# The first MLP's down projection in seven products, with the residual kept in DRAM

## The chip, the cores and the metric

The kernel runs on one core of a Trainium2 chip. The metric is device time in microseconds (us) for one execution; lower is better. Five engines work side by side and meet through semaphores: TensorE (PE; its weight loads are listed apart as PEld), VectorE (DVE), ScalarE (ACT), GpSimd (POOL) and SyncE (SP), which issues most transfers.

## What is computed

A trunk of two layers over 512 tokens of width 1024, all in float32. Each layer is a mixer (latent attention in layer 0, gated linear attention, "GLA", in layer 1) and an MLP, each added to the residual stream `x`; a last RMS norm follows. The change is in the MLP of layer 0.

```python
D_MODEL = 1024; SEQ = 512; D_FF = 4 * D_MODEL

def sq_relu_mlp(xn, w_up, w_down):
    hid = jnp.square(jax.nn.relu(xn @ w_up))
    return hid @ w_down

for i in range(DEPTH):
    ...
    x = x + mix.astype(x.dtype)
    x = x + sq_relu_mlp(rms_norm(x, norm_mlp[i]), mlp_w_up[i], mlp_w_down[i]).astype(x.dtype)
return rms_norm(x, final_norm)
```

## The kernel before

**Precision.** A float32 matrix is split into a rounded high part (ACT copies it, line 104) and a low part (DVE subtracts, line 107). A product takes three matmuls: high x high, high x low, low x high. Weights pass through `piece`, which has three buffers for high parts (`wh`) and three for low (`wl`).

**The stream.** `xT` is one SBUF tile, `xall`, of 128 partitions x 8 x 512: the residual with features on the partitions and tokens along the row.

**MLP of layer 0, `mlp` (from line 799).** The 4096 hidden features are done in eight blocks of 512. The first block's up projection, `up`, is plain: 96 matmuls of 512 columns. The other seven are made by `up_fast`: the 1024 x 512 weight block and the activations are cut into 2 x 2 quadrants, and seven products of sums of quadrants (Winograd's form of Strassen's scheme) replace eight. Each product is 8 matmuls of 512 columns (line 891; high and low activations side by side) and 8 of 256 (line 892). The down projection of every block, `down`, is plain: 8 output tiles, 12 matmuls of 512 columns each (lines 112 to 114), each tile added to `xT` by DVE (line 843). `down` of block b is woven into `up_fast` of block b + 1 through `others`. So seven periods of one fast up step and one plain down block follow `up`, and the eighth `down` stands alone at the end; there `nxt.add` scales each finished tile for the next norm, and GLA begins.

**MLP of layer 1, `mlp_last` (from line 972).** Here both projections use seven products. A step, `step`, alternates up products (24 matmuls of 256 columns, line 1108) with down products (12 of 512 columns, line 1117). A down product's output has tokens on the partitions. Partial results are summed in five tiles: S11, S12, SU, S21, which lie over `xall`, and S5. Since they lie over the residual, `residual` first turns it by 32 TensorE transposes (line 1061) into the sums. The quadrants of activations and their combinations T1 to T4 (`quadrants`) are made in four buffers of the pool `comb`, then rounded into tiles `T`; the buffers then serve for weights. `home` says which buffer a weight quadrant gets: d11, d12, d22 and so on are quadrants of `w_down`, dS1 and dS3 sums of two (the second added in flight by an accumulating transfer from POOL), S1 such a sum of `w_up`, A1 and A2 halves of `w_up` in the buffers `wraw`. `fetch` issues the loads. The step's parts of hidden quadrants are split into four pairs of tiles, `parts_room`. After seven steps the eighth block is plain, with the output norm woven in.

**Order.** A scheduler orders each engine's instructions at build time from the program; in a queue nothing overtakes. PSUM has eight banks: in `mlp` z and y (two each), three for `down` and one; in `mlp_last` four for up products (`u`) and d and e (two each) for down products.

Of the kernel before, what the change touches and what calls it, by code (L numbers as in the profile page):

```python
# [50 lines left out]
def trunk_kernel(ctx: ExitStack, tc: tile.TileContext, t_in: dict, out: bass.AP):  # L51
# [47 lines left out]
    def f(ap):  # L99
        return ap.bitcast(F32)  # L100
# [698 lines left out]
    def mlp(layer, nrm, tag, nxt):  # L799
        w_up, w_dn = t_in["mlp_w_up"][layer], t_in["mlp_w_down"][layer]  # L800
        X = nrm.out
        NB = FF // FB

        es = ExitStack()
        fast = es.enter_context(tc.tile_pool(name=f"fast{layer}", bufs=1, reuse_waits="tile"))

        def up():
            hid = []
            for c in range(2):
                raw = col_chunk(w_up, c * 256, 256)  # L810
                w = [piece(raw[:, :, j * P : (j + 1) * P], ND, P) for j in range(2)]
                ps_ = split_banks("zy"[c])
                if c == 0:
                    a_pair(ps_, w, nrm)
                else:
                    for j in range(2):
                        a_type(ps_[j], w[j], X)
                for j in range(2):
                    r = tmp()
                    DVE.scalar_tensor_tensor(r, ps_[j], 0.0, nrm.rstd, ALU.max, ALU.mult)  # L820
                    q = tmp()
                    ACT.activation(q, r, AF.Square)
                    hi, lo = slot(tag), slot(tag)
                    ACT.activation(hi, q, AF.Copy)
                    quad["hid"] = DVE.tensor_tensor(lo, q, f(hi), ALU.subtract).ins
                    hid.append((hi, lo))
            return hid

        def down(b, hid):
            for c in range(2):  # L830
                src = w_dn[b * FB : (b + 1) * FB, c * 512 : (c + 1) * 512].rearrange("(k p) n -> p k n", p=P)
                if c == 0 and b < NB - 1:
                    raw = fast.tile([P, 4, 512], F32, tag="raw", name=uname("raw"))
                    SP.dma_start(raw, src)
                else:
                    raw = load(src, 4, 512)
                for g in range(2):
                    w = piece(raw[:, :, g * 256 : (g + 1) * 256], 4, 256)
                    for j in range(2):
                        m = c * 4 + g * 2 + j  # L840
                        p = bank("b")
                        a_type(p, w, hid, cols=slice(j * P, (j + 1) * P))
                        DVE.tensor_tensor(xT[m], p, xT[m], ALU.add)
                        if b == NB - 1:
                            nxt.add(m, xT[m])
                        yield

        first, second = slice(0, TH), slice(TH, S)  # L850
        KH = ND // 2

        def comb():
            return fast.tile([P, KH, 256], F32, tag="comb", bufs=4, name=uname("comb"))

        quad = {}

        def quadrants():
            lead, trail = range(KH), range(KH, ND)
            quad["11"] = [nrm.parts[k][:, :, first] for k in lead]  # L860
            quad["21"] = [nrm.parts[k][:, :, first] for k in trail]
            quad["22"] = [nrm.parts[k][:, :, second] for k in trail]
            t1, t2, t3, t4 = comb(), comb(), comb(), comb()
            for k in lead:
                g1, g2 = (gcol(nrm.g, nrm.g0 + j) for j in (k, k + KH))
                u, v = xT[k], xT[k + KH]
                ACT.activation(t3[:, k], u[:, second], AF.Copy, scale=g1)
                DVE.scalar_tensor_tensor(t3[:, k], v[:, second], g2, t3[:, k], ALU.mult, ALU.subtract)
                DVE.scalar_tensor_tensor(t2[:, k], u[:, first], g1, t3[:, k], ALU.mult, ALU.add)
                DVE.scalar_tensor_tensor(t4[:, k], v[:, first], g2, t2[:, k], ALU.mult, ALU.subtract)  # L870
                DVE.scalar_tensor_tensor(t1[:, k], v[:, second], g2, t2[:, k], ALU.mult, ALU.subtract)
            for name, t in (("T2", t2), ("T3", t3), ("T1", t1), ("T4", t4)):
                parts = fast.tile([P, KH, 2, TH], F32R, tag=name, name=uname(name))
                split(t, parts[:, :, 0], parts[:, :, 1])
                quad[name] = [parts[:, k] for k in lead]

        def up_fast(b, others):
            raw = [col_chunk(w_up, b * FB + c * 256, 256) for c in range(2)]
            a11, a12 = raw[0][:, :KH], raw[0][:, KH:]
            a21, a22 = raw[1][:, :KH], raw[1][:, KH:]  # L880
            halves = [(slot(tag), slot(tag)) for _ in range(4)]


            def product(t, a, q, start):
                w = piece(a, KH, 256)
                for j in range(2):
                    o = t[:, j * 512 : (j + 1) * 512]
                    for k in range(KH):
                        wh, wl = cut(w, slice(None), k, slice(j * P, (j + 1) * P))
                        x = quad[q][k]  # L890
                        PE.matmul(o.rearrange("p (h t) -> p h t", h=2), wh, x, start=start and k == 0, stop=False, skip_group_check=True)  # L891
                        PE.matmul(o[:, :TH], wl, x[:, 0], start=False, stop=k == KH - 1, skip_group_check=True)  # L892

            def parts(t):
                v = t.rearrange("p (j h t) -> p h j t", j=2, h=2)
                return v[:, 0], v[:, 1]

            def by_tile(v):
                return v.rearrange("p (j t) -> p j t", j=2)


            def total(t, term=None):
                high, low = parts(t)
                r = tmp()
                if term is None:
                    ACT.activation(by_tile(r), low, AF.Copy)
                else:
                    DVE.tensor_tensor(by_tile(r), low, by_tile(term), ALU.add)
                DVE.tensor_tensor(by_tile(r), high, by_tile(r), ALU.add)
                return r  # L910


            def finish(c, half, tk):
                c3 = by_tile(c)
                DVE.scalar_tensor_tensor(c3, c3, 0.0, nrm.rstd[:, tk].unsqueeze(1).to_broadcast([P, 2, TH]), ALU.max, ALU.mult)
                ACT.activation(c, c, AF.Square)
                for j in range(2):
                    hi, lo = halves[2 * half + j]
                    split(c3[:, j], hi[:, tk], lo[:, tk])

            z, y = two_banks("z"), two_banks("y")
            product(z, a11, "11", True)
            others(1)
            p1 = total(z)
            s1, s2 = comb(), comb()
            DVE.tensor_tensor(s1, a21, a22, ALU.add)
            DVE.tensor_tensor(s2, s1, a11, ALU.subtract)
            product(y, a12, "21", True)
            c11 = total(y, p1)
            product(z, s2, "T2", False)  # L930
            others(2)
            u = total(z)
            finish(c11, 0, first)
            s4 = comb()

            with tc.issue_after(quad["hid"]) if b == 1 else nullcontext():
                DVE.tensor_tensor(s4, a12, s2, ALU.subtract)
                DVE.tensor_tensor(a21, a11, a21, ALU.subtract)
            product(z, a21, "T3", False)
            v = total(z)  # L940
            y = two_banks("y")
            product(y, s1, "T1", True)
            others(1)
            c22 = total(y, v)
            product(y, s4, "22", False)
            product(z, a22, "T4", False)
            finish(c22, 1, second)
            c12 = total(y, u)
            finish(c12, 0, second)
            c21 = total(z)  # L950
            finish(c21, 1, first)
            others(4)
            return halves

        hid = up()
        quadrants()
        for b in range(NB):
            if b + 1 < NB:
                tiles = down(b, hid)

                def others(n):
                    for _ in range(n):
                        next(tiles)

                hid = up_fast(b + 1, others)
                continue
            es.close()
            for _ in down(b, hid):
                pass
# [890 lines left out]
```

## Time and profile before

| | us |
|---|---|
| median of 3 runs | 1069.12 (1068.77 to 1069.77) |
| profiled execution | 1070.06 |
| its span, first to last instruction | 1068.4 |
| layer 0: first up block ends | 205.59 |
| layer 0: last plain down block begins | 495.48 |
| layer 1: first up block ends | 761.33 |
| layer 1: last plain block begins | 1039.82 |

The granted TensorE clock is 0.999 of full on the mean. By DMA queue, packets, megabytes and the share of the sixteen DMA engines' time:

```profile
q1 hardware_dynamic: 89376, 106.22, 30.6%
q0 software_dynamic: 11200, 14.68, 8.6%
```

q1 is SP's queue, q0 POOL's. A line number in the profile is a line of the kernel before; lines 104 and 107 are in a helper, so tiles tell such rows apart (`wh<-wraw`, `wh<-comb`). A matmul's duration includes its way through the array, and consecutive matmuls overlap.

### The profile page before, as it was taken

The numbers are of one execution on the slowest core, as the hardware profiler recorded it, in microseconds if no ns is written. First come the engines' busy times: TensorE is split into PE (matmuls) and PEld (weight loads), VectorE is DVE, ScalarE is ACT, GpSimd is POOL, SyncE is SP. The second block draws the span as 40 slices with busy tenths as digits, with TensorE's granted clock in tenths as the row PEclk, the third lists the DMA queues.
The fourth block names the chain that finished last, engine by engine and source line by source line (L and its number), as shares of the span: only waits on it lengthen the run. The fifth ranks groups of instructions, "written<-read, shape, count | busy, mean of one in ns | idle before, by whom it ended". The sixth has DMA issues, their size and how long they took to land.

```text
span 1068.4 us, 14750 instructions
## 1 busy us (share of the span) xinstructions
PE 1058.9 (99%) x5626; PEld 908.2 (85%) x5626; DVE 868.1 (81%) x1384; ACT 630.2 (59%) x1010; POOL 78.5 (7%) x100
## 2 busy tenths in 40 slices
PE   9999999999999999999999999999999999999997
PEld 8888888888888888888888888878889999999985
DVE  7899977987978878877778389478789989989993
ACT  7667654553444444445445475665567767777784
POOL 8310002000000000000000000000011011010000
PEclk9999999999999999999999999999999999999999
DMA  7311223142233233214222221343576786696622
GB/s 228 89 50 40 80 83 114 40 157 80 79 124 113 79 111 114 92 41 154 73 98 62 97 64 47 116 101 127 138 208 149 196 236 137 180 252 142 176 82 79
DMA packets 102742, 123.67 MB, mean 116 GB/s; under 512 B 8368, under 2 KB 74416, under 8 KB 102672
## 3 DMA queue, kind: packets, MB, share of 16 engines
q1 hardware_dynamic: 89376, 106.22, 30.6%
q0 software_dynamic: 11200, 14.68, 8.6%
q10 hardware_dynamic: 2096, 1.84, 0.5%
q8 instruction: 44, 0.72, 0.3%
q14 instruction: 26, 0.21, 0.1%
HBM read 120.37 MB, written 2.10 MB: 115 GB/s over the span
## 4 chain that ended last, share of the span: by engine, by line
PE 93%; DVE 3%; ACT 2%; DMA 1%; issue 1%; ACTq 0%; DVEq 0%
PE ps L112 15%; PE ps L114 15%; PE ps L113 15%; PE ps L1108 13%; PE ps L1117 13%; PE ps L891 8%; PE ps L892 4%; PE ps L1504 2%; PE ps L129 1%; PE ps L1284 1%; PE ps L408 1%; DMA comb<-in_mlp_w_down_dram 1%; PE ps L1631 1%; DVE wl L107 1%; DVE T L999 0%
## 5 line engine op out<-in xcount | busy, mean ns | idle before, releaser
L104 ACT ACTIVATE wh<-wraw 128x1024 fp32r<-128x1024 f32 x139 | 146.6, 1058 | 153.3 <-PE ps L113 73.8
L112 PE MATMUL ps<-set,wh 128*128 128x512 f32 x536 | 209.1, 391 | 0.5 <-ACT set L1673 0.3
L113 PE MATMUL ps<-set,wh 128*128 128x512 f32 x536 | 209.2, 391 | 0.0
L114 PE MATMUL ps<-set,wl 128*128 128x512 f32 x536 | 208.7, 390 | 0.0
L107 DVE TENSOR_TENSOR wl<-wraw,wh 128x1024 fp32r<-128x1024 f32 x139 | 169.6, 1222 | 34.8 <-ACT wh L104 34.6
L1117 PE MATMUL ps<-wh,set 128*128 128x512 f32 x392 | 129.3, 390 | 0.0
L104 ACT ACTIVATE wh<-comb 128x1024 fp32r<-128x1024 f32 x77 | 81.8, 1062 | 75.0 <-PE ps L891 40.9
L107 DVE TENSOR_TENSOR wl<-comb,wh 128x1024 fp32r<-128x1024 f32 x77 | 94.2, 1223 | 36.2 <-ACT wh L104 36.1
L112 PEld LDWEIGHTS ps<-set,wh 128*128 128x128 f32 x536 | 100.6, 188 | 22.2 <-ACT wh L104 1.0
L114 PEld LDWEIGHTS ps<-set,wl 128*128 128x128 f32 x536 | 100.6, 188 | 21.6 <-DVE wl L107 0.4
L113 PEld LDWEIGHTS ps<-set,wh 128*128 128x128 f32 x536 | 100.7, 188 | 19.7
L1117 PEld LDWEIGHTS ps<-wh,set 128*128 128x128 f32 x392 | 73.7, 188 | 14.4
L1108 PE MATMUL ps<-T,wh 128*128 128x256 f32 x448 | 79.9, 279 | 0.0
L891 PE MATMUL ps<-T,wh 128*128 128x512 f32 x224 | 78.7, 391 | 0.0
L1117 PE MATMUL ps<-wl,set 128*128 128x512 f32 x196 | 76.8, 392 | 0.0
L1108 PEld LDWEIGHTS ps<-T,wh 128*128 128x128 f32 x448 | 70.3, 188 | 2.2
L892 PE MATMUL ps<-T,wl 128*128 128x256 f32 x224 | 63.1, 282 | 0.0
L1108 PE MATMUL ps<-T,wl 128*128 128x256 f32 x224 | 62.6, 279 | 0.5 <-DVE wl L107 0.5
L1108 PE MATMUL ps<-set,wh 128*128 128x256 f32 x336 | 61.3, 283 | 0.0
L891 PE MATMUL ps<-set,wh 128*128 128x512 f32 x168 | 60.0, 397 | 0.0
L112 PE MATMUL ps<-wh,set 128*128 128x512 f32 x144 | 58.6, 407 | 0.0
L114 PE MATMUL ps<-wh,set 128*128 128x512 f32 x144 | 56.8, 396 | 0.0
(416 smaller groups left out, 2205.6 us busy)
## 6 DMA issues: line engine op xcount, KB each, us to landing
wraw<-in_mlp_w_up_dram SPq DMA_DIRECT2D x32, 1024.0 KB, 5.4
comb<-in_mlp_w_down_dram SPq DMA_DIRECT2D x39, 512.0 KB, 4.7
wraw<-in_gla_w_in_dram SPq DMA_DIRECT2D x12, 1024.0 KB, 5.2
wraw<-in_mlp_w_down_dram SPq DMA_DIRECT2D x9, 1024.0 KB, 5.1
raw<-in_mlp_w_down_dram SPq DMA_DIRECT2D x7, 1024.0 KB, 5.0
comb<-in_mlp_w_down_dram POOLq DMA_DIRECT2D x14, 512.0 KB, 7.3
wraw<-in_mla_w_o_dram SPq DMA_DIRECT2D x4, 1024.0 KB, 5.3
wraw<-in_gla_w_o_dram SPq DMA_DIRECT2D x4, 1024.0 KB, 5.5
```

The lines of the kernel that those rows point to most:

```text
L104: order(ACT.activation(hi, src, AF.Copy))
L107: lo_eng.tensor_tensor(lo, src, f(hi), ALU.subtract)
L112: PE.matmul(psum, wh, xh, start=start, stop=False)
L113: PE.matmul(psum, wh, xl, start=False, stop=False)
L114: PE.matmul(psum, wl, xh, start=False, stop=stop)
L129: PE.transpose(psum, src, ident[: src.shape[0], : src.shape[0]])
L408: PE.matmul(p, w[:, i, j * P : (j + 1) * P], x, start=start, stop=stop)
L891: PE.matmul(o.rearrange("p (h t) -> p h t", h=2), wh, x, start=start and k == 0, stop=False, skip_group_check=True)
L892: PE.matmul(o[:, :TH], wl, x[:, 0], start=False, stop=k == KH - 1, skip_group_check=True)
L1108: PE.matmul(o, a_, x_, start=start and j == 0 and k == 0 and n == 0, stop=k == KH - 1 and n == 2, skip_group_check=True)
L1117: PE.matmul(o, x_, w_, start=start and k == 0 and n == 0, stop=k == 1 and n == 2, skip_group_check=True)
L1504: PE.matmul(p[:, t - t0], k[:, t * P : (t + 1) * P], moving[:, t], start=True, stop=True)
```

## The change

`mlp` is removed, and `mlp_last`, now called `mlp`, serves both layers; it is told by `nxt` that a norm follows. For layer 0:

- PSUM has the layout of layer 1 (`"quad"`).
- `residual` is not called. SP stores `xall` in a DRAM tile, `x_kept`, of 128 x 8 x 512, ahead of dS3's load. In the first step the sums are not added to but written (`opening`).
- In the last step, four loads bring `x_kept` back, two tiles at a time, into `comb` buffers, and two load the last block's down weights into `wraw`.
- The last block is plain, with features on the partitions again. The parts of the hidden quadrants are laid in `room` with all 512 tokens of a tile in a row. For every output tile four transposes turn the sums' 128 x 128 pieces into its bank, and 12 matmuls of 512 columns add the block's product onto them; DVE adds the kept residual, and `nxt.add` follows.

For both layers, d11 and dS3 exchange their first buffers.

```diff
-    def mlp(layer, nrm, tag, nxt):
...
-    def mlp_last(layer, nrm):
+    def mlp(layer, nrm, nxt=None):
...
+        if nxt:
+            dram = es.enter_context(tc.tile_pool(name=f"spill{layer}", bufs=1, space=bass.MemoryType.DRAM))
+            x_kept = dram.tile([P, ND, S], F32, name="x_kept")
...
-        home = {"S1": 0, "dS1": 1, "d11": 2, "d12": 3, "dS3": 4, "d22": 5}
+        home = {"S1": 0, "dS1": 1, "d11": 4, "d12": 3, "dS3": 2, "d22": 5}
...
         def step(b, q, r, after):
+            opening = b == 0 and nxt is not None
...
             def add(total, t):
-                DVE.tensor_tensor(total, t, total, ALU.add)
+                if opening:
+                    ACT.activation(total, t, AF.Copy)
+                else:
+                    DVE.tensor_tensor(total, t, total, ALU.add)
...
             down_product(d, d11, parts_of_quad(q11), True)
-            e = begun(d)
+            if opening:
+                ACT.activation(S11, d, AF.Copy)
+            e = two_banks("e") if opening else begun(d)
...
-            down_product(e, d12, parts_of_quad(q21), False)
-            add(S11, e)
+            down_product(e, d12, parts_of_quad(q21), opening)
+            DVE.tensor_tensor(S11, e, S11, ALU.add)
...
-            onto("d", S21, d22, parts_of_quad(q21, -1.0))
+            onto("d", S21, d22, parts_of_quad(q21, -1.0), opening)
...
-        residual()
+        if not nxt:
+            residual()
         for name in ("S1", "dS1", "d11", "A1", "d12", "dS3", "A2", "d22"):
-            fetch(0, name)
+            if name == "dS3" and nxt:
+                with tc.issue_after(queued.ins):
+                    SP.dma_start(x_kept, xall)
+            queued = fetch(0, name)
...
+        def before_next(name):
+            if name in ("d11", "S1", "d12", "dS3"):
+                t = by_k(comb(home[name]), 2)
+                SP.dma_start(t, x_kept[:, 2 * len(kept) : 2 * len(kept) + 2])
+                kept.append(t)
+            if name in ("A1", "A2"):
+                last_raw.append(load(down_cols(len(last_raw)), 4, 512))
+            if name == "dS1":
+                DVE.tensor_tensor(S12, S12, S5, ALU.add)
...
+        if nxt:
+            room = [parts_room[(turn[0] + k) % 4] for k in range(4)]
+            for h, th in ((0, 0), (0, 1), (1, 1), (1, 0)):
+                for j in range(2):
+                    split(q[h][th][:, j * TH : (j + 1) * TH], *cut(room[2 * h + j], slice(None), (first, second)[th]))
+            DVE.scalar_tensor_tensor(S21, S21, -1.0, SU, ALU.mult, ALU.subtract)
+            DVE.scalar_tensor_tensor(SU, SU, -1.0, S5, ALU.mult, ALU.subtract)
+            for c in range(2):
+                ps_ = [bank("u") for _ in range(4)] if c == 0 else [p for tag in "ed" for p in split_banks(tag)]
+                for j, p in enumerate(ps_):
+                    for t in range(NT):
+                        o = t % 2 * 512 + j * P
+                        src = (S11, S12, S21, SU)[2 * c + t // 2][:, o : o + P]
+                        PE.matmul(p[:, t * P : (t + 1) * P], src, ident, start=t == 0, stop=False, is_transpose=True, skip_group_check=True)
+                for j, p in enumerate(ps_):
+                    if j % 2 == 0:
+                        w = piece(last_raw[c][:, :, j * P : (j + 2) * P], 4, 256)
+                    for k in range(4):
+                        wh, wl = cut(w, slice(None), k, slice(j % 2 * P, (j % 2 + 1) * P))
+                        for n, (a, x) in enumerate(((wh, room[k][0]), (wh, room[k][1]), (wl, room[k][0]))):
+                            PE.matmul(p, a, x, start=False, stop=k == 3 and n == 2, skip_group_check=True)
+                    m = 4 * c + j
+                    DVE.tensor_tensor(xT[m], p, kept[m // 2][:, m % 2], ALU.add)
+                    nxt.add(m, xT[m])
+            es.close()
+            return
...
-    psum_layout(True)
-    mlp(0, n_mlp0, "B", n_mix1)
+    psum_layout("quad")
+    mlp(0, n_mlp0, n_mix1)
     psum_layout(False)
...
-    mlp_last(1, n_mlp1)
+    mlp(1, n_mlp1)
```

Three places show what the engines are given now. (Rows: line, operation, tile written <- tiles read, shape, semaphores waited for; lines after the change are those of the changed kernel.) First SP's queue at the start of layer 0. Before, with the two halves of `w_up` for the first fast step last:

```order
L834 DMA raw_2392<-in_mlp_w_down_dram 128x4x512 [waits DVE_49,PE_49,Pool_49]
L134 DMA wraw_2054<-in_mla_w_o_dram 128x8x256 [waits DMAHW6_49,DVE_49]
L134 DMA wraw_2159<-in_mlp_w_up_dram 128x8x256 [waits DMAHW7_49,DVE_49]
L134 DMA wraw_2247<-in_mlp_w_up_dram 128x8x256 [waits DMAHW1_49,DVE_49]
L134 DMA wraw_2358<-in_mlp_w_up_dram 128x8x256 [waits DMAHW2_49,DVE_49]
L134 DMA wraw_2360<-in_mlp_w_up_dram 128x8x256 [waits DMAHW3_49,DVE_49]
```

After, where wraw_2372 is A1, comb_2370 d11, comb_2374 d12, comb_2377 dS3, wraw_2380 A2 and comb_2383 d22:

```order
L134 DMA wraw_2372<-in_mlp_w_up_dram 128x8x256 [waits DMAHW3_49,DVE_49]
L926 DMA comb_2370<-in_mlp_w_down_dram 128x2x512 [waits DVE_49]
L926 DMA comb_2374<-in_mlp_w_down_dram 128x2x512 [waits DVE_49]
L1054 DMA x_kept<-xT 128x4096 [waits DMAHW0_49]
L926 DMA comb_2377<-in_mlp_w_down_dram 128x2x512 [waits DMAHW1_49,DVE_49,Pool_49]
L134 DMA wraw_2380<-in_mlp_w_up_dram 128x8x256 [waits DMAHW4_49,DVE_49]
L926 DMA comb_2383<-in_mlp_w_down_dram 128x2x512
```

The store stands between d12's load and dS3's. Second, ACT in the first step of layer 0. Before, at the first fast up step (wh_2442 and wh_2506 are weights of the following products):

```order
L906 ACTIVATE tmp_2412<-ps_532_2370 128x512 [waits PE_49]
L104 ACTIVATE wh_2442<-comb_2416 128x1024
L104 ACTIVATE wh_2476<-raw_2392 128x1024 [waits DVE_49,PE_49]
L104 ACTIVATE wh_2506<-wraw_2360 128x1024 [waits DVE_49,DMAHW5_49,PE_49,Activation_49]
L906 ACTIVATE tmp_2494<-ps_532_2370 128x512 [waits PE_49]
```

After; the row of line 985 is the copy of the first down product to S11, which lies in `xT`, and wh_2491 is the weights of the product on T2:

```order
L104 ACTIVATE wh_2471<-comb_2374 128x1024 [waits DMAHW7_49,PE_49]
L980 ACTIVATE ps_2414<-ps_2385 128x512 [waits PE_49]
L104 ACTIVATE set_2170<-set_2163 128x512 [waits DVE_49,PE_49]
L985 ACTIVATE xT<-ps_540_2416 128x1024 [waits DMAHW0_49,PE_49]
L104 ACTIVATE wh_2491<-wraw_2372 128x1024
```

The copy waits for a transfer (the store) and for TensorE, and T2's weights are queued behind it. Third, TensorE at the end of the last step of layer 0, after the change (ps_902 is bank d, ps_5124 to ps_5127 are four banks `u`, the sets are room pieces):

```order
L948 MATMUL ps_902_5087<-wh_5089,set_2171 128x512
L1122 MATMUL ps_5124<-ident,xT 128x128 x2
L1122 MATMUL ps_5124<-ident,xT 128x128 [waits DVE_49]
L1122 MATMUL ps_5124<-ident,xT 128x128
L1122 MATMUL ps_5125<-ident,xT 128x128 x4
L1122 MATMUL ps_5126<-ident,xT 128x128 x4
L1122 MATMUL ps_5127<-ident,xT 128x128 [waits DVE_49]
L1122 MATMUL ps_5127<-ident,xT 128x128 x3
L1129 MATMUL ps_5124<-set_2172,wh_5144 128x512 [waits Activation_49]
L1129 MATMUL ps_5124<-set_2173,wh_5144 128x512
```

The 16 transposes of the first four tiles stand between the last down product and the plain block; the 16 of the other four stand between the block's two halves. Before, the eighth `down` followed the seventh fast step directly. From GLA on, each engine's order is unchanged, but for SP's at the start of layer 1, where d11's load now stands ahead of d12's, d22's and dS3's, and for the lines' numbers.

More of the change, by code (lines that the diff above doesn't have):

```diff
@@ L796, in out_proj @@
                 add(m, p)
-    def mlp(layer, nrm, tag, nxt):
[L800 to L969, printed above, removed]
@@ L1095, in fetch @@
             }[name]
-            SP.dma_start(t, q(b, *plain))
+            first_part = SP.dma_start(t, q(b, *plain))
             if more:
                 POOL.dma_start(t, q(b, *more), accum_op=ALU.add)
+            return first_part
         def up_product(t, a, q, start):
@@ L1224, in rounded, with down_cols @@
                     last[c].append((parts[:, 0], parts[:, 1]))
+        def down_cols(c):
+            return w_dn[(NB - 1) * FB :, c * 512 : (c + 1) * 512].rearrange("(k p) n -> p k n", p=P)
+        def before_next(name):
[7 more added lines that the diff above has]
+                DVE.tensor_tensor(S12, S12, S5, ALU.add)
         def at_the_end(name):
@@ L1245, in after @@
                 if final:
-                    return at_the_end(name)
+                    return before_next(name) if nxt else at_the_end(name)
                 new = NEXT[name]
```

4 lines of the change are left out of this document (2 added, 2 removed).

## The prediction, made before the change was run

> **What bounds the kernel now.** I read the page's busy shares first, then busy time by stretch, then single matmuls on the timeline, and last the chain of waits. The page:
>
> ```profile
> PE 1058.9 (99%) x5626; PEld 908.2 (85%) x5626; DVE 868.1 (81%) x1384; ACT 630.2 (59%) x1010; POOL 78.5 (7%) x100
> ```
>
> TensorE never rests, but a row's duration is not its price. In the timeline of TensorE (start, duration, line), at the first seven-product up step of layer 0:
>
> ```profile
> 205.59 0.39 PE L891 MATMUL ps<-set,wh 128*128 128x512 f32 x1
> 205.82 0.28 PE L892 MATMUL ps<-set,wl 128*128 128x256 f32 x1
> 205.93 0.40 PE L891 MATMUL ps<-set,wh 128*128 128x512 f32 x1
> ```
>
> The first matmul is shown with 0.39 us, yet the next starts 0.23 us later and the one after that 0.11 us later: matmuls overlap. The price is the distance between starts, some 0.23 us for 512 columns and 0.12 us for 256. So what counts is how many columns each MLP block streams, and whether TensorE gets them without a gap. Stretches (length, busy time and count by engine, clock, DMA share, GB/s): seven blocks of layer 0 (from the matmul at 205.59 to the start of the last plain block at 495.48), and the same work of layer 1 from 783.28 to 1039.82.
>
> ```profile
> 205.59:495.48 289.89, 289.89 (x1457) 246.32 (x1456) 237.98 (x317) 132.03 (x194) 0.99 (x2) 1.00 0.30 99
> 783.28:1039.82 256.54, 256.54 (x1657) 233.93 (x1657) 231.81 (x257) 189.41 (x238) 28.80 (x23) 1.00 0.70 181
> ```
>
> No TensorE idle in either, at full clock. Layer 0 takes 289.89 / 7 = 41.41 us for a block. In layer 1 the chain of waits shows what a seven-product step is made of (start, length, what):
>
> ```profile
> 783.28 2.80 PE ps L1108 x24
> 786.08 2.75 PE ps L1117 x12
> ...
> 1037.07 2.75 PE ps L1117 x12
> 1039.82 14.03 PE ps L1284 x60
> ```
>
> An up product of 24 matmuls with 256 columns, then a down product of 12 with 512, alternating to the end with nothing between them: 46 pairs in 256.54 us, 5.577 us each. A step has seven pairs, 39.04 us. DVE is 90% busy there (231.81 of 256.54) and still does not hold TensorE up.
>
> **The change, part by part.**
>
> *Seven steps of layer 0.* Now a block is 152 matmuls of 512 columns (96 down, 56 up) and 56 of 256; after, 84 of 512 and 168 of 256. In columns that is 92,160 against 86,016, and 41.41 against 39.04 us. Layer 0 runs the code that layer 1 runs now, and the order of instructions within a step is the same; its 49 pairs cost 49 x 5.577 = 273.3 us in place of 289.89: **-16.6**. Bounds: 5.55 to 5.61 us for a pair (both spellings of the up product occur in the chain, 2.80 and 2.87), so ±1.5.
>
> On a rule of the skill: the Trainium skill, "TensorE: Matmul & The Clock Gate", section "Back-to-back issue gap", gives a sustained roofline in streams of weight load and matmul of about 131 ns at 512 columns and 81 ns at 128; by that a 256-column matmul would cost, as an estimate between the two, 98 ns, three quarters of a 512, and the step would grow from 25.4 to 27.5 us. The rows above have 0.23 and 0.12 us, a half; the same section's isolated gap (N/2.4 + 2.5 ns) says a half too, and by that trace the sum goes.
>
> *Sums turned into the banks.* 32 transposes are added to layer 0, the same count and shape as layer 1's residual:
>
> ```profile
> 761.33 1.91 PE L1061 MATMUL ps<-ident,xT 128*128 128x128 f32 x16
> 763.00 0.48 PE L1108 MATMUL ps<-set,wh 128*128 128x256 f32 x2
> ...
> 764.61 2.01 PE L1061 MATMUL ps<-ident,xT 128*128 128x128 f32 x16 [0.41 <-ACT xT L1065]
> 766.37 0.36 PE L1108 MATMUL ps<-set,wl 128*128 128x256 f32 x1
> ```
>
> From start to the next start 1.67 and 1.76 us: **+3.4**. The 96 matmuls of the last plain block stay, in another place.
>
> *Entry into the first step.* Layer 0 has no gap there now. Layer 1 has one before the T2 product, and layer 0 gets it with the code. The chain:
>
> ```profile
> 771.09 0.02 ACT set L104
> 771.11 0.52 issue
> 771.63 1.01 ACT ps L1125
> 772.63 0.99 ACT wh L104
> ...
> 773.64 1.24 DVE wl L107
> ```
>
> When the first down product ends, ACT must split a part, copy the bank (1.01) and only then round T2's weights (0.99), and DVE subtracts (1.24); TensorE has one up product for cover. In the timeline:
>
> ```profile
> 773.99 0.40 PE L1108 MATMUL ps<-T,wh 128*128 128x256 f32 x2
> 774.92 0.39 PE L1108 MATMUL ps<-T,wl 128*128 128x256 f32 x1 [0.53 <-DVE wl L107]
> ```
>
> Two matmuls (0.24) in 0.93: 0.7 lost. In the opening step the copy goes to S11 and not to a bank, at the same place with the same shape, and T2's weights stand right behind it: **+0.7** (0 to 1.3).
>
> *The residual put aside.* The 2.10 MB store of xT to DRAM is hidden if it lands before S11 is first written over; ACT's copy of S11 waits for it. SP issues it third in a row. T3 and T2 are rounded in layer 0 already now:
>
> ```profile
> 187.67 1.28 DVE L107 TENSOR_TENSOR T<-comb,T 128x1024 fp32r<-128x1024 f32 x1
> 190.33 3.48 DVE L107 TENSOR_TENSOR T<-comb,T 128x1024 fp32r<-128x1024 f32 x3
> ```
>
> The first frees d11's buffer at 188.95, the second d12's at about 191.5; the store follows at 191.9. S11 is due when up product, down product and one split are over: 205.59 + 2.87 + 2.75 + some 0.8 = 212.0. So 20 us are there. The trace has no 2 MB store. What the engines move at full load shows at layer 1's start, where five loads and an accumulation crowd:
>
> ```profile
> 750.00:755.00 5.00, 5.00 (x24) 4.14 (x23) 4.83 (x6) 3.10 (x6) 0.00 (x0) 1.00 0.89 213
> 755.00:760.00 5.00, 5.00 (x24) 4.14 (x23) 2.51 (x3) 1.78 (x4) 0.00 (x0) 1.00 1.03 302
> ```
>
> d11, d12 and the store are 3.15 MB: 10.4 to 14.8 us from 188.9, and 2 us to land (a 64 KB copy takes that), 201 to 206: in time. If all that is under way shared alike (dS3, d22, A2 and an accumulation, 5.8 MB at 213 GB/s) it would be 216, 4 us late. The only stores of the trace are the outputs:
>
> ```profile
> out_dram<-xT SPq DMA_DIRECT2D x4, 256.0 KB, 2.6
> rstd<-rstd SPq DMA_DIRECT2D x4, 64.0 KB, 2.0
> ```
>
> Eight of them one after the other would end at 212.7. Bounds 0 to +4; I take **0**, since the queue of SP goes in order in this trace: the load issued at 749.28 landed before the 1 MB issued at 753.86, for which POOL waited until 761.73.
>
> ```profile
> 749.28 8.86 DMA comb<-in_mlp_w_down_dram
> ...
> 761.73 1.28 POOL L1088 DMA_DIRECT2D wraw<-in_mlp_w_up_dram  x1 [12.00 <-DMA wraw<-in_mlp_w_up_dram]
> ```
>
> The Trainium skill, "DMA: Bandwidth & Descriptors", section "Queues, rings and completion order", says that each DMA engine consumes a ring in order and takes turns only between queues; by that only POOL's accumulation shares with the store, and nothing is added. Behind the store in SP's queue stand dS3, A2 and d22, due 20 us later at the fifth to last products. POOL gets 21 accumulating loads, as layer 1 has. The four reads back (512 KB) and the two loads of the last block go into buffers free one to five products before, in a step that fetches nothing else.
>
> *Exit into the plain block.* TensorE runs the last d22 product, 16 transposes (1.7 us), and needs the last room pieces at the tenth matmul behind (2.0 us): 3.7 us. ACT needs a split (0.37), the copy of S21 (1.01), a split; DVE turns S21 (1.23) and subtracts (0.48): about 3.2 us. Their kin:
>
> ```profile
> 737.40 0.48 DVE L1045 SCALAR_TENSOR_TENSOR comb<-xT,gains,comb 128x256 f32<-128x256 f32 x1
> ...
> 762.91 0.73 ACT L1030 ACTIVATE set<-tmp 128x256 f32<-128x256 f32 x2 [0.56 <-DVE tmp L1028]
> ...
> 1040.23 1.01 ACT L1136 ACTIVATE xT<-ps 128x1024 f32<-128x1024 f32 x1
> 1041.27 1.23 DVE L1258 TENSOR_TENSOR xT<-xT 128x1024 f32<-128x1024 f32 x1 [0.23 <-ACT xT L1136]
> ```
>
> Hidden with half a us to spare; I take **+0.2** (0 to +1.4). Then GLA starts on xT in the order it has now.
>
> *Layer 1.* d11 moves to T3's buffer, freed first, and its load goes ahead of three others. ACT waited for it:
>
> ```profile
> 758.22 1.06 ACT L104 ACTIVATE wh<-comb 128x1024 fp32r<-128x1024 f32 x1 [4.74 <-DMA comb<-in_mlp_w_down_dram]
> ```
>
> TensorE was in its plain block until 761.33, so that wait cost nothing itself; behind it ACT and DVE ran late, and 0.41 us of TensorE's idle at 764.61 hangs on that: **-0.3** (-0.6 to 0).
>
> **Sum**: -16.6 + 3.4 + 0.7 + 0 + 0.2 - 0.3 = **-12.6 us**. The profiled execution has 1070.06 us with a span of 1068.4, and the runs' median is 1069.12; the difference is taken from the median: **1056.5 us**.
>
> **The rivals.**
>
> *The store is late, or a joint stalls.* ACT stands at S11's copy with all its splits behind it, and after one up product TensorE waits for T2's weights, 1:1. For it: the DMA is at its ceiling there. Against: order in the queue. 2 to 5 us: 1058.5 to 1061.5.
>
> *The same place, slower than before.* The store would have to land 12.6 + 2.1 = 14.7 us late, after 226.7: 2.10 MB in 34.8 us, 60 GB/s. The output stores do 256 KB in 2.6 us, 98 GB/s with their landing in it. At half of that (42.8 us, 22.7 late) the time would be 1079.
>
> *256 columns cost more than half of 512.* If the shown durations were prices:
>
> ```profile
> L1108 PE MATMUL ps<-T,wh 128*128 128x256 f32 x448 | 79.9, 279 | 0.0
> L891 PE MATMUL ps<-T,wh 128*128 128x512 f32 x224 | 78.7, 391 | 0.0
> ```
>
> a step would go from 152 x 391 + 56 x 279 to 84 x 391 + 168 x 279 ns, 6% more: 41.41 to 44.0, and with the transposes 1069.1 + 18.0 + 3.4 = 1090.5. Layer 1's pairs speak against it: by durations 12 x 391 + 24 x 279 ns would be 11.4 us, and they took 5.577. The skill's roofline named above points the same way.
>
> *It brings little.* DVE or the doubled DMA (share 0.30 to 0.70) holds layer 0's steps to 41 us: 1069 + 0 to 1070. Layer 1 carries the same load on both at 39.04.
>
> **Chances.** Forecast (1055.0 to 1058.2) 0.76; late store or joint (up to 1062) 0.16; between that and no change 0.02; little 0.02; slower by the store 0.03, by 256 columns 0.01. The range 1055.0 to 1060.6 holds the first and most of the second. A run of this kernel tells 0.2%, 2.1 us: faster 0.94, the same 0.02, slower 0.04.
>
> **What would show it.** Right: pairs of 2.8 and 2.75 us in layer 0, seven steps in 273 us; the store landing by 206 and no DMA wait at ACT's S11 copy; 0.7 us lost before T2; transposes of 1.7 us each group and no gap before GLA; d11 of layer 1 landing some 5 us sooner. Wrong: TensorE idle released by ACT at T2 for over a us, pairs above 5.65 us, or a hole between the last down product and the plain block.

## The result, and the profile after

The changed kernel runs in 1061.44 us (median of 4 runs, 1059.98 to 1061.83), the kernel before beside it in 1069.39 (1068.77 to 1069.77): a ratio of 0.9924, 95% interval 0.9907 to 0.9941. That is 8.0 us faster, where 12.6 were forecast, and 0.8 us above the range. The profiled execution has 1061.28 us, a span of 1059.6 and a mean granted clock of 0.997.

The page's first part, after:

```profile
PE 1047.6 (99%) x5966; PEld 915.1 (86%) x5966; DVE 876.7 (83%) x1340; ACT 698.5 (66%) x1074; POOL 113.5 (11%) x128
```

TensorE has 340 more matmuls and is still 99% busy. The two profiled spans, 1068.4 and 1059.6 us, are 8.8 us apart; the table shows where these lie:

| stretch | before | after | difference |
|---|---|---|---|
| to the end of layer 0's first up block | 205.59 | 205.49 | -0.10 |
| seven steps of layer 0 | 289.89 | 274.14 | -15.75 |
| last block, to the norm's matmul in GLA (line 264) | 28.73 | 36.45 | +7.72 |
| GLA, and layer 1's first up block | 237.12 | 237.02 | -0.10 |
| layer 1: residual and seven steps | 278.49 | 278.00 | -0.49 |
| last block and output | 28.58 | 28.50 | -0.08 |

The two MLPs in busy time by stretch (the columns as in the prediction):

```profile
205.49:479.63 274.14, 273.63 (x1766) 249.27 (x1766) 243.06 (x268) 199.40 (x252) 32.15 (x27) 1.00 0.71 181
753.10:1031.10 278.00, 277.47 (x1798) 252.95 (x1797) 249.39 (x276) 204.32 (x258) 29.86 (x24) 1.00 0.67 171
```

Layer 0 now looks like layer 1: half a microsecond of TensorE idle in 274, DVE 89% busy, the DMA engines at 0.71. All that came less than forecast is in the third row of the table. The chain of waits there:

```profile
476.88 2.76 PE ps L948 x12
479.63 1.75 PE ps L1122 x16
481.38 10.91 PE ps L1129 x48
492.29 1.75 PE ps L1122 x16
494.03 6.34 PE ps L1129 x27
500.46 1.07 ACT wh L104
501.56 1.16 DVE wl L107
502.72 0.72 DVE set L250
503.44 0.60 DVE acc L239
504.05 0.61 DVE xT L1131
504.70 4.57 PE ps L1129 x12
509.28 0.23 PE ps L112
```

The last down product, 16 transposes and the first half of the plain block (48 matmuls, 10.91 us) join without a gap. The second half has the same 48 matmuls, from 494.03 to 509.28: 15.25 us. Its chain leaves TensorE at 500.46: ACT rounds weights of GLA, DVE makes their low part (line 107), scales tile 5 for the next norm (line 250) and adds its squares to the norm's sum (line 239), and only then adds tile 6 to the residual (line 1131). TensorE's matmuls for tile 7 wait for that. In TensorE's timeline:

```profile
502.01 0.39 PE L1129 MATMUL ps<-set,wl 128*128 128x512 f32 x1
504.70 1.22 PE L1129 MATMUL ps<-set,wh 128*128 128x512 f32 x2 [2.30 <-DVE xT L1131]
505.72 0.63 PE L1129 MATMUL ps<-set,wl 128*128 128x512 f32 x1
506.15 1.05 PE L1129 MATMUL ps<-set,wh 128*128 128x512 f32 x2
```

Starts lie 2.69 us apart in place of 0.23, so 2.46 are lost. Then matmuls come 0.43 us apart until 508.2, twice the usual distance. The busy time by stretch names it: the granted clock, the last figure but two, is 0.72.

```profile
504.00:510.00 6.00, 5.30 (x16) 4.27 (x17) 2.69 (x5) 2.11 (x3) 0.00 (x0) 0.72 0.53 173
```

Before, the whole plain block ran without a gap at full clock, with DVE 17.05 us busy of 21.52:

```profile
495.48:517.00 21.52, 21.52 (x96) 17.83 (x95) 17.05 (x23) 11.89 (x17) 0.00 (x0) 1.00 0.32 100
```

The order of TensorE's instructions tells what tile 7 waits for. In the second half the four output tiles are halves of two tiles of two banks, e (tiles 4, 5) and d (6, 7). The two rows are the last matmul of tile 6 and, behind it, the first of tile 7, whose wait is for DVE's addition of tile 6 to the residual:

```
L1129 MATMUL ps_922_5228<-set_2170,wl_5288 128x512
L1129 MATMUL ps_922_5228<-set_2172,wh_5287 128x512 [waits DVE_49]
```

Tile 5 waits for DVE's addition of tile 4 in the same way. There the order has four matmuls of tile 6 in between, and no gap shows; behind tile 6 the block has nothing left to put in between. In the first half, where each tile has a single bank `u`, no tile's first matmul waits for DVE's read of the tile before.

### The profile page after: what moved, and what is told of

Same layout as the page of the kernel before. It is cut to its first block, busy times and chain, and to the rows that moved or that the text cites. A ratio compares the mean times of both kernels' runs of the same rounds, so it can differ in the third digit from the quotient of the medians.

```text
span 1059.6 us, 15597 instructions
## 1 busy us (share of the span) xinstructions
PE 1047.6 (99%) x5966; PEld 915.1 (86%) x5966; DVE 876.7 (83%) x1340; ACT 698.5 (66%) x1074; POOL 113.5 (11%) x128
## 4 chain that ended last, share of the span: by engine, by line
PE 95%; ACT 2%; DVE 2%; issue 0%; ACTq 0%; DVEq 0%
PE ps L939 26%; PE ps L948 25%; PE ps L112 10%; PE ps L114 10%; PE ps L113 10%; PE ps L1129 2%; PE ps L1384 2%; PE ps L129 1%; PE ps L1164 1%; PE ps L408 1%; PE ps L1511 1%; DVE wl L107 1%; ACT wh L104 0%; PE ps L1648 0%; PE ps L671 0%
## 5 line engine op out<-in xcount | busy, mean ns | idle before, releaser
L948 PEld LDWEIGHTS ps<-wh,set 128*128 128x128 f32 x784 | 147.3, 188 | 28.8
L939 PE MATMUL ps<-T,wh 128*128 128x256 f32 x896 | 159.9, 279 | 0.0
L948 PE MATMUL ps<-wl,set 128*128 128x512 f32 x392 | 153.7, 392 | 0.0
L939 PEld LDWEIGHTS ps<-T,wh 128*128 128x128 f32 x896 | 140.6, 188 | 4.4
L939 PE MATMUL ps<-set,wh 128*128 128x256 f32 x672 | 122.6, 283 | 0.0
L112 PE MATMUL ps<-set,wh 128*128 128x512 f32 x280 | 109.3, 392 | 0.7 <-ACT set L1553 0.3
L113 PE MATMUL ps<-set,wh 128*128 128x512 f32 x280 | 109.4, 391 | 0.0
L114 PE MATMUL ps<-set,wl 128*128 128x512 f32 x280 | 109.0, 390 | 0.0
L939 PE MATMUL ps<-set,wl 128*128 128x256 f32 x336 | 95.2, 283 | 0.0
L939 PEld LDWEIGHTS ps<-T,wl 128*128 128x128 f32 x448 | 84.2, 188 | 1.5 <-DVE wl L107 1.4
L948 PEld LDWEIGHTS ps<-wl,set 128*128 128x128 f32 x392 | 73.7, 188 | 11.6
```

The lines of the kernel that those rows point to most:

```text
L112: PE.matmul(psum, wh, xh, start=start, stop=False)
L113: PE.matmul(psum, wh, xl, start=False, stop=False)
L114: PE.matmul(psum, wl, xh, start=False, stop=stop)
L939: PE.matmul(o, a_, x_, start=start and j == 0 and k == 0 and n == 0, stop=k == KH - 1 and n == 2, skip_group_check=True)
L948: PE.matmul(o, x_, w_, start=start and k == 0 and n == 0, stop=k == 1 and n == 2, skip_group_check=True)
```

## The experiments

All are made from the changed kernel; times are medians, each beside the kernel before on the same chip.

| kernel | us | ratio to before, 95% interval |
|---|---|---|
| tiles alternate | 1057.59 (1057.02 to 1058.89) | 0.9892, 0.9878 to 0.9905 |
| single banks | 1058.49 (1058.28 to 1058.96) | 0.9900, 0.9885 to 0.9915 |
| hole filled | 1059.79 (1059.30 to 1060.02) | 0.9910, 0.9897 to 0.9924 |
| hole half filled | 1059.91 (1059.82 to 1060.24) | 0.9910, 0.9897 to 0.9924 |
| the changed kernel again | 1060.88 (1060.19 to 1062.22) | 0.9919, 0.9904 to 0.9934 |
| copy later | 1061.01 (1059.38 to 1061.51) | 0.9920, 0.9908 to 0.9932 |
| three stores | 1061.43 (1061.14 to 1061.82) | 0.9925, 0.9912 to 0.9937 |
| old buffers | 1063.73 (1061.93 to 1065.94) | 0.9948, 0.9935 to 0.9962 |
| five stores | 1067.57 (1065.30 to 1069.20) | 0.9980, 0.9970 to 0.9989 |
| tiles alternate, copy later | 1057.30 (1056.47 to 1057.47) | 0.9884, 0.9870 to 0.9897 |

**Tiles alternate.** The second half's tiles in the order 4, 6, 5, 7.

```diff
-                for j, p in enumerate(ps_):
-                    if j % 2 == 0:
-                        w = piece(last_raw[c][:, :, j * P : (j + 2) * P], 4, 256)
+                ws = {}
+                for j in ((0, 1, 2, 3), (0, 2, 1, 3))[c]:
+                    p = ps_[j]
+                    if j // 2 not in ws:
+                        g = j // 2 * 2
+                        ws[j // 2] = piece(last_raw[c][:, :, g * P : (g + 2) * P], 4, 256)
+                    w = ws[j // 2]
```

> Second half of layer 0's plain block with its four output tiles taken in the order m = 4, 6, 5, 7, so that two neighbours in time never share a two-bank tile. The changed kernel takes 15.2 us from 494.03 to 509.2 for these 48 matmuls; 48 with no gap take 10.9. Theory A (TensorE waits because the wait is kept for the whole two-bank tile, so m = 7 stands behind DVE's read of m = 6): the read now has another tile's 12 matmuls (2.75 us) as cover, the gap of 2.46 us goes, and with it the low clock behind it (0.72 over 6 us, some 1.7 us): 11 us for the half, 4 us less, near 1057.4, all of the second half's matmuls 0.23 us apart. Rival B (DVE and ACT are simply late at this joint): the hole moves to the next tile or to the first matmuls of the attention's projection; within 1 us of 1061.4.

Its chain of waits:

```profile
494.30 10.89 PE ps L1133 x48
505.19 0.23 PE ps L112
```

The second half takes 10.89 us, and GLA follows at once. The time is 3.9 us below the changed kernel's, as the theory had it. DVE and ACT do the same work as before, so they are not too slow for this joint: each read only needs another tile's matmuls beside it.

**Single banks.** The second half in four `u` banks, in the old order.

```diff
-                ps_ = [bank("u") for _ in range(4)] if c == 0 else [p for tag in "ed" for p in split_banks(tag)]
+                ps_ = [bank("u") for _ in range(4)]
```

> The second half goes into the four single banks that the first half used, tiles in the old order; no two-bank tile is left in it. Theory A: no tile waits for another's read, so the hole of 2.46 us before the last 12 matmuls goes as in the alternating order; what is new is that the four groups of transposes wait for DVE's read of the tile of the first half in the same bank (that of m = 3 comes some 1 to 2.5 us after its last matmul), so 2 to 4 us less than the changed kernel, 1057.4 to 1059.4. Rival B: the hole stays before the last 12 matmuls or moves behind them, and the transposes' wait comes on top: 1061.4 to 1063.

The 48 matmuls run from 494.37 to 505.1 without a gap. What is left is one wait behind them, in the timeline (0.83 us idle, 1.22 between starts):

```profile
506.78 0.47 PE L112 MATMUL ps<-set,wh 128*128 128x512 f32 x1 [0.83 <-DVE xT L1131]
```

GLA's second output needs a bank that DVE has not yet read. So 3.0 us are won, within the theory's 2 to 4. The alternating order has no such wait, and its median is 0.9 us lower, though the runs of the two kernels overlap.

**Hole filled, and half filled.** Ten spare matmuls of 512 columns, in a second kernel five, ahead of tile 7's; the order is otherwise the changed kernel's.

```diff
+                    if c == 1 and j == 3:
+                        spare = bank("u")
+                        for n in range(10):
+                            PE.matmul(spare, w[0][:, 0, 0:P], room[0][0], start=n == 0, stop=n == 9)
```

> The order is the changed kernel's, but ten matmuls of 512 columns on a spare bank (2.3 us) stand in TensorE's queue ahead of the 12 matmuls of m = 7; their result is not used. They fill the hole of 2.46 us and take away nothing of the wait. Theory: part of the loss, some 1.7 us, is the clock that the hole costs (12 matmuls 0.43 us apart in place of 0.23): the granted clock stays 1.00, the last 12 take 2.75 us, and the time is 1.5 to 1.7 us below the changed kernel, 1059.8. Rival (the clock drops there for another reason, or the 12 matmuls are slow because DVE and ACT use the memory then): the low clock stays and the time is that of the changed kernel, 1061.4, or up to 0.5 more.

> As the filled hole, with five spare matmuls in place of ten: 1.13 us of the hole of 2.46 are filled, 1.2 to 1.3 us stay. In the kernel with single banks a hole of 1.2 us before the attention's second group left the matmuls 0.23 us apart. Theory (the clock falls only after a hole longer than that): clock 1.00 as with ten, the 12 last matmuls in some 2.8 us, 1059.8. Rival (any hole of over a us costs the clock): the 12 take 4.4 us, 1061.4.

With ten, the chain of waits (line 1127 is the spare work):

```profile
494.36 8.37 PE ps L1133 x36
502.73 2.27 PE ps L1127 x10
505.03 3.01 PE ps L1133 x12
```

The spare work fills the wait and does not shorten it, but the 12 matmuls behind it take 3.0 us in place of 4.57, and the time falls by 1.65 us. So a part of the loss is the clock alone. With five, 1.17 us of idle remain, the granted clock stays at 1.00 (from 504 to 510), and the time is the same as with ten:

```profile
504.84 0.73 PE L1133 MATMUL ps<-set,wh 128*128 128x512 f32 x2 [1.17 <-DVE xT L1135]
```

**The changed kernel again.** No edit.

> The changed kernel once more, to see how its own time spreads. Theory (the hole of 2.46 us lowers the clock in some executions and not in others, as in the kernel with the old buffers, whose hole of the same size left the clock at 1.00): times between 1059.5 and 1062 with two groups, those with a mean clock of 0.999 some 1.5 us below those with 0.997; the median 1061.4 as before. Rival (the hole always costs the clock): all runs within 0.5 us of 1061.4.

Its profiled execution (1060.19 us) has the same hole and no low clock; a row of its chain, and of its busy time by stretch:

```profile
505.19 3.02 PE ps L1129 x12
```

```profile
504.00:510.00 6.00, 4.81 (x21) 4.00 (x22) 4.02 (x6) 3.18 (x5) 0.00 (x0) 1.00 0.55 178
```

The eight runs of this kernel fall in two groups: 1059.98, 1060.19 and 1060.26 with a mean clock of 0.999 or 1.000, and 1061.28 to 1062.22 with 0.997 or 0.998, some 1.5 us apart. The wait alone costs 2.8 us (the second half takes 13.69 there, from 494.52 to 508.21, and 10.91 without a gap); the clock costs 1.5 more in five runs of eight, as their mean clocks have it (only two of the eight have a trace). The kernels with filled holes, at 1059.30 to 1060.24, lie with the first group.

**Copy later.** In the opening step ACT's copy of the first down product to S11, and DVE's addition, come after the product on T2.

```diff
...
-            if opening:
-                ACT.activation(S11, d, AF.Copy)
...
-            DVE.tensor_tensor(S11, e, S11, ALU.add)
+            if not opening:
+                add(S11, e)
...
             up_product(z, a11, "T2", False)
+            if opening:
+                ACT.activation(S11, d, AF.Copy)
+                DVE.tensor_tensor(S11, e, S11, ALU.add)
```

> In the opening step ACT's copy of the first down product to S11 and DVE's addition to it come behind T2's up product in place of before it, so that T2's weights are not rounded behind the copy (1.01 us). Theory (the 0.67 us lost at T2 are this copy standing ahead of the weights): the gap before T2's second product group goes, 0.7 us less, 1060.7, and the hole at the exit stays as it is. Rival (T2's weights are late because of DVE's additions, or the d11 product now waits for the copy): no change, or the 0.7 us appear one product later.

In its chain, the first products of layer 0 and the last:

```profile
205.73 2.87 PE ps L939 x24
208.61 2.75 PE ps L948 x12
211.35 5.19 PE ps L939 x42
...
476.63 2.76 PE ps L948 x12
479.39 1.75 PE ps L1124 x16
```

The products on either side of T2's weights join now. The seven steps take 273.66 us in place of 274.14: 0.48 won, not 0.67. The median fell by 0.43, which the spread of the runs doesn't tell from nothing; the chain does.

**Old buffers.** Only `home` is set back: d11 in buffer 2, dS3 in 4.

```diff
-        home = {"S1": 0, "dS1": 1, "d11": 4, "d12": 3, "dS3": 2, "d22": 5}
+        home = {"S1": 0, "dS1": 1, "d11": 2, "d12": 3, "dS3": 4, "d22": 5}
```

> Only the buffers of d11 and dS3 are as in the kernel before, in both layers (d11 in T2's place 2, dS3 in 4). Theory: the 0.49 us that layer 1's steps are shorter come from d11's earlier load; undone, ACT waits for that load again at layer 1's start and TensorE is idle for some 0.4 us before the second group of transposes; and in layer 0, where d11 is issued ahead of the store, the store starts some 2.5 us later (it is issued behind d11, and T2's old buffer comes free later) and still lands before S11's copy: 0.3 to 0.6 more than the changed kernel, 1061.9. Rival (layer 1's gain is chance): no change there. Where the store would land after the copy: 2 us and more on top.

The cost is 2.3 us, not 0.3 to 0.6. Part of it is where the theory had it, in layer 1: residual and steps take 278.84 us, 0.84 more, with this wait ahead of the second group of transposes:

```profile
757.84 2.01 PE L891 MATMUL ps<-ident,xT 128*128 128x128 f32 x16 [0.80 <-ACT xT L895]
```

The larger part is in layer 0, and I had it wrong: I took d11 to be issued ahead of the store. Its old buffer comes free last of the three, so the scheduler put dS3's load ahead of the store and d11's, the first that is needed, behind it. The chain, and the rows of ACT and TensorE that follow from it:

```profile
193.65 11.84 DMA comb<-in_mlp_w_down_dram
```

```profile
205.57 1.06 ACT L104 ACTIVATE wh<-comb 128x1024 fp32r<-128x1024 f32 x1 [3.02 <-DMA comb<-in_mlp_w_down_dram]
```

```profile
217.40 0.39 PE L939 MATMUL ps<-T,wl 128*128 128x256 f32 x1 [2.05 <-DVE wl L107]
```

A load of 0.5 MB behind a store of 2.1 MB lands 11.84 us after its issue. Steps end at 482.30 in place of 479.63; 0.48 of that lies before them (their first matmul starts at 205.81 in place of 205.33), and the steps themselves take 2.2 us more. At the exit this execution had the usual hole (2.30 us) with the clock at 1.00, so its span is only 1.9 us longer.

**Three stores, five stores.** The residual is stored to three places, then to five; the computation is the same.

```diff
...
-                    SP.dma_start(x_kept, xall)
+                    for kept_at in (x_kept, x_more, x_last):
+                        SP.dma_start(kept_at, xall)
```

> The residual is stored three times, to three places in DRAM, one behind the other in SP's queue; the computation is the same. One store took 9.1 us from issue to landing (191.28 to 200.4), and the copy that writes S11 over the residual starts at 211.46. Theory (the store is hidden only because it lands 11 us ahead of the copy; the queue goes in order; past the deadline TensorE loses time 1:1): the third lands at 191.3 + 3 x 9.1 = 218.6, ACT's copy waits for it, and with T2's weights behind that copy TensorE stands for some 6 to 7 us more than now, with some 1.7 us of low clock after it; dS3, A2 and d22 come 18 us later, which for dS3 (needed near 233) is just in time: 1067 to 1071. Rival (stores overlap, so that three take hardly longer than one, or the copy doesn't wait for them): within 1 us of 1061.4.

Three stores cost nothing. SP issued them at 191.71, 192.22 and 192.69; the profile's list of DMA issues has, last in each row, the time to landing:

```profile
x_kept<-xT SPq DMA_DIRECT2D x1, 2048.0 KB, 9.0
x_more<-xT SPq DMA_DIRECT2D x1, 2048.0 KB, 13.9
x_last<-xT SPq DMA_DIRECT2D x1, 2048.0 KB, 18.3
```

They landed at 200.7, 206.1 and 211.0, in order, some 5 us apart and not 9.1, so much of the first one's 9 us was not its own transfer (two loads are ahead of it). And the scheduler had set ACT's copy back behind T2's weights, to 212.84, which takes away the gap at T2 too. So the deadline was not broken, and this run doesn't test what a late store costs. Hence five:

> The residual is stored five times, to five places in DRAM. Three stores left the deadline unbroken: they landed at 200.7, 206.1 and 211.0, some 5 us apart, and ACT's copy to S11 stood at 212.84. By that the fourth lands near 216 and the fifth near 221. Theory (in order in the queue, and the copy waits for all of them): the copy stands until 221, and the product that writes on the bank that it copies, due at 216.7 with three stores, starts near 222: 5 to 6 us of idle TensorE in the opening step, with 0 to 1.7 us of low clock after it: 1066.5 to 1069 (the changed kernel at 1061.4). Rival (stores share the engines with everything, the last lands near the fourth's time): at most 1 us, 1062.5.

The 6.1 us came as expected, but by another way; the profiled execution, at 1065.47, is among the fastest of its ten. The last store landed at 220.5; the copy to S11 (line 986) stood at 227.29 by the order and waited for nothing:

```profile
225.81 1.06 ACT L104 ACTIVATE wh<-wraw 128x1024 fp32r<-128x1024 f32 x1 [3.34 <-PE ps L940]
...
227.29 1.00 ACT L986 ACTIVATE xT<-ps 128x1024 f32<-128x1024 f32 x1
```

The scheduler had put other products ahead of the one that overwrites the copied bank. In that order, as I read it, ACT waits for a weight buffer that TensorE still reads (3.34 us in the first row) and TensorE then for ACT and for DVE behind it: 3.3 us idle in four holes from 219 to 228, and a low clock beside them. Together these make up most of the 5.7 us by which the seven steps are longer than in the changed kernel's trace (279.80 us, from 205.38 to 485.18). The first two holes, and the busy time by stretch:

```profile
220.57 0.51 PE L940 MATMUL ps<-T,wh 128*128 128x256 f32 x2 [0.84 <-ACT wh L104]
221.83 0.38 PE L940 MATMUL ps<-T,wl 128*128 128x256 f32 x1 [0.75 <-DVE wl L107]
```

```profile
218.00:224.00 6.00, 4.40 (x26) 3.76 (x25) 4.33 (x5) 3.01 (x4) 1.05 (x1) 0.91 0.98 345
224.00:230.00 6.00, 4.31 (x21) 3.57 (x20) 2.45 (x2) 2.48 (x3) 2.65 (x3) 0.80 1.08 331
```

What a late store costs in the changed kernel's own order stays open.

**Tiles alternate, copy later.** Both edits together.

> The alternating order of the second half and the later copy of the opening step together. The alternating order alone ran at 1057.59, 3.9 us below the changed kernel; the later copy alone took 0.48 us from the seven steps (205.73 to 479.39 in place of 205.49 to 479.63). Theory (two stalls in different places, nothing shared): they add up, 4.4 below the changed kernel, 1057.1 (1056.6 to 1057.6), with TensorE without a hole from 205 to the attention's norm. Rival (one hides the other): not below 1057.6.

The steps run from 205.48 to 479.16, and the chain ends the block thus:

```profile
480.91 10.92 PE ps L1135 x48
491.83 1.75 PE ps L1124 x16
493.58 10.90 PE ps L1135 x48
504.47 0.23 PE ps L112
```

Both gains are in this trace, the steps at 273.68 us and the block's end without a hole. The median is 4.1 us below the changed kernel and 12.5 below the kernel before beside it (1069.81), the lowest here and close to what the prediction gave the change itself; the 0.3 us to the alternating order alone is within the spread of the runs.

## Why the prediction was off

The step that failed is the exit: "Hidden with half a us to spare; I take **+0.2** (0 to +1.4)." It cost 4.2 us in the profiled execution (7.72 of the table less 3.50 of transposes), and would have cost 2.8 with the clock held. What that step looked at, the room pieces at the start of the plain block, was as it said: no gap from 476.88 to 494.03. It stopped there, and the sentence on the transposes, "The 96 matmuls of the last plain block stay, in another place", set the rest at nothing. The place was the cost. Before, the block's tiles rotate through three single banks; after, its second half sits two tiles to a two-bank tile, so a tile's matmuls start only when DVE has read its neighbour, and DVE comes to tile 6 through three other instructions. The alternating order (the same banks, no hole) and single banks (the tiles in the old order, no hole there) show the mechanism from two sides; the filled holes show that 1.5 of it was the clock. The rival of a stalled joint, with its chance of 0.16, had the right size but named another joint, T2's weights behind a late store.

The other steps:

- *Seven steps and entry*, forecast 273.3 + 0.7 = 274.0 us: 274.14. Pairs are 2.80 or 2.87 and 2.75 to the end. The sustained roofline that the prediction quotes from the Trainium skill, "TensorE: Matmul & The Clock Gate", section "Back-to-back issue gap", did not hold in layer 0 either: 24 matmuls of 256 columns in 2.80 us are 0.117 us each, half of the 0.23 at 512.
- *The gap at T2*, forecast 0.7, is there by the mechanism named:

```profile
211.46 1.01 ACT L985 ACTIVATE xT<-ps 128x1024 f32<-128x1024 f32 x1
212.37 1.05 ACT L104 ACTIVATE wh<-wraw 128x1024 fp32r<-128x1024 f32 x1
```

```profile
213.82 0.40 PE L939 MATMUL ps<-T,wh 128*128 128x256 f32 x2
214.73 0.39 PE L939 MATMUL ps<-T,wl 128*128 128x256 f32 x1 [0.51 <-DVE wl L107]
```

  Two matmuls take 0.91 us in place of 0.24, as in layer 1; taking the copy away gave back 0.48.
- *Transposes*, forecast 3.4: two groups of 1.75.
- *The store*, forecast 0 with a landing between 201 and 206: issued at 191.28, landed at 200.4. The copy at 211.46 waits for no transfer. The 302 GB/s that the prediction took for full load is not the most that its trace shows: the loads at the start of the kernel before moved 369 GB/s from 5 to 10 us. And 256 KB in 2.6 us are 101 GB/s, not 98. Neither changes the forecast. The Trainium skill, "DMA: Bandwidth & Descriptors", section "Queues, rings and completion order", has a ring taken in order; the three stores that land one after the other, and d11 behind the store in the kernel with the old buffers, agree.
- *Layer 1*, forecast -0.3: -0.49, and 0.84 when the buffers are set back. ACT no longer waits for d11 but for TensorE:

```profile
747.62 1.07 ACT L104 ACTIVATE wh<-comb 128x1024 fp32r<-128x1024 f32 x1 [2.37 <-PE ps L113]
```

  The prediction gave the exchange of buffers no part in layer 0. It has the larger part there: without it d11's load stands behind the store, and the seven steps take 2.2 us longer.

## What to carry to other kernels

When work "stays, in another place", price the place: how many output tiles share one tracked tile of PSUM, and which engine must have read one before the next is written. Put two tiles that share it apart in time, so that the read has another tile's matmuls beside it; here a changed order of four tiles gave 3.9 us for nothing. A hole on TensorE can cost more than its length, by the clock behind it, and a change that puts a long transfer in a queue needs a look at what the scheduler then puts behind it.

## What the runs showed of the hardware

- A hole of 2.3 us (idle in the row) lowered the granted clock in some executions and left it at 1.00 in others of the same kernel; holes of 1.17 and 0.83 us left it at 1.00 where a profile shows them, and the four runs with the 1.17 us hole lie within 0.42 us. Short holes close together did lower it: in the kernel with five stores TensorE is idle for 0.84 and 0.75 us between 219.4 and 221.8, and its matmuls of 256 columns then start some 0.21 us apart from 223 to 225.6, in place of 0.12, ahead of the next hole. The Trainium skill, "TensorE: Matmul & The Clock Gate", section "What's actually happening", has half rate as the low state, and a free-running window of some 3.4 us of which a whole one has to be idle. The half rate agrees: 0.43 us between starts in place of 0.23, and 0.72 over 6 us is, as an estimate, (1 - 0.72) x 6 / 0.5 = 3.4 us at half rate, about one such window. That a whole window must be idle does not agree, since the hole was 2.3 us, and in the kernel with five stores the two holes together were 1.6. A free-running window fits that the same hole costs the clock in one run and not in the next, though no run here sets its phase.
- Stores to DRAM moved faster than forecast: 2.1 MB each 5 us once under way. In the kernel with five stores, stores and loads together moved 433 GB/s from 205 to 212; the loads at the start of the kernel before moved 369 from 5 to 10:

```profile
205.00:212.00 7.00, 7.00 (x48) 6.47 (x47) 6.37 (x7) 4.41 (x7) 0.00 (x0) 1.00 1.02 433
```
